# Who builds the gated one-hot rows: half of ScalarE's instructions in the gates stage are replaced by VectorE instructions of two operations

## The chip, the cores and the metric

The kernel runs on one core of one Trainium2 chip, and the metric is the device time of a run in microseconds. The engines named below are TensorE (PE in the profile, PEld its weight loads), VectorE (DVE), ScalarE (ACT), GpSimd (POOL, which issues the indirect gathers) and SyncE (SP, which issues the other transfers). Each engine works through its own list of instructions in order and waits for the others by semaphores.

## The reference, cut to what matters

The program is one decoder block for 1024 tokens of width 1024: a time-mixing and an attention branch, then a feed-forward layer with 16384 experts, of which each token uses 8 x 16 = 128. The change lies in that last layer:

```python
e1 = jnp.take_along_axis(i1, ci // PK_TOPK, axis=-1)
e2 = jnp.take_along_axis(i2, ci % PK_TOPK, axis=-1)
ids = (e1 * PK_NKEYS + e2).reshape(T, PK_HEADS * PK_TOPK)
gates = jax.nn.softmax(vals, axis=-1).reshape(T, PK_HEADS * PK_TOPK)
...
act = jnp.einsum('ced,cd->ce', u_tab[idc], xc)
act = jax.nn.gelu(act, approximate=False) * gc
return jnp.einsum('ce,ced->cd', act, v_tab[idc])
```

An expert is a pair (e1, e2) of numbers from 0 to 127. A token's 128 gates can be written as a 128 x 128 matrix over (e2, e1), zero where the token doesn't use the expert.

## The kernel before

The 1024 tokens are eight tiles of 128. The experts' part of the first four tiles goes by gathering, that of the last four by dense products.

**Gathered tiles, the peers.** `peer` (L806) takes one tile. For each of its 128 choices POOL gathers 128 rows of 4 KB (L792, 512 KB in all) from table u, and DVE multiplies and sums them (L814). Then the same follows from table v (L821). Such a gather with its DVE instruction is called a peer here. There are 1024 of them, one after another in POOL's list, through five buffers called uv. They depend on nothing in the work below, so the framework that schedules the program at build time sets them between the other work.

**Dense tiles.** `choose` (L711) finds the 128 experts and gates of one tile, mostly on DVE. `gates` (L824) turns them into the gate matrices. Tokens are taken in groups of four. For each group DVE makes the one-hot rows of e1 for all four tokens (`oh`, L833). For every eight tokens DVE makes the one-hot rows of e2 (`ohb`, L837, bf16). ACT multiplies each token's e2 row by its gate (`ohg`, L842). PE multiplies `ohg` by `oh` (`gb`, L843), one 128 x 128 product for each token, which the profile shows as two records. ACT moves the group's four products from PSUM to `st` (L844). After eight groups SP stores `st`, 2 MB, in `gd_s` (L847). `st` has two buffers, the PSUM bank of `gb` has two, `ohg` two and `oh` four. A tile has 32 groups, the four tiles 128 groups and 512 `ohg` instructions.

Beside the gates, `ahead` (L854) computes the first 16 of 128 dense products with table u (`ua` on PE, with weights `whi` made by ACT in L153 and `wlo` made by DVE in L154).

`dense` (L861) then walks through the 128 rows of experts. It reads the gates of four rows (`gt`, 1 MB), applies gelu and gate (`gw`, L883 and L884) and makes the products with table v (`yk`, `yr`). DVE takes part in each step (L154, L176, L884, L904). Peers stand between these steps. When the dense steps are over, the peers that are left run alone.

So the list of each engine is: mixing, the choice of experts, the gates stage (from the first `oh` to the first `gw`), the dense stage, and a tail.

Of the kernel before, what the change touches and what calls it, by code (L numbers as in the profile page):

```python
# [13 lines left out]
AF = mybir.ActivationFunctionType  # L14
OP = mybir.AluOpType
# [3 lines left out]
P = 128  # L19
# [28 lines left out]
def body(ctx: ExitStack, tc: tile.TileContext, ins, out, dbg=None):  # L48
    nc = tc.nc
# [15 lines left out]
    def abank(name):  # L65
        return ps.tile([P, 512], F32, name=name, tag="ab", bufs=2)
# [31 lines left out]
    def const(name, shape, dt=F32):  # L98
        t = kp.tile(shape, dt, name=name)
        nc.sync.dma_start(t, ins[name])  # L100
        return t
# [15 lines left out]
    eye_row = const("eye_row", [P, P])  # L117
# [705 lines left out]

    def gates(sp, a, sl, eye8):  # L824

        e1, g = sl[:, 0:P], sl[:, 2 * P:3 * P]
        e2 = sl[:, 3 * P:].bitcast(BF)[:, 0:P]
        nc.scalar.activation(e2, sl[:, P:2 * P], AF.Copy)
        for q in range(0, P, 32):
            st = sp.tile([P, P // CE, 32, CE], F32, name="st", bufs=2)  # L830
            for t in range(0, 32, 4):
                o1 = sp.tile([P, 4, P], F32, name="oh", bufs=4)
                nc.vector.tensor_tensor(o1, eye_row[:, None, :].to_broadcast([P, 4, P]),  # L833
                                        e1[:, q + t:q + t + 4, None].to_broadcast([P, 4, P]), op=OP.is_equal)
                if t % 8 == 0:
                    o2 = sp.tile([P, P, 8], BF, name="ohb", bufs=2)
                    nc.vector.tensor_tensor(o2, eye8, e2[:, None, q + t:q + t + 8].to_broadcast([P, P, 8]),  # L837
                                            op=OP.is_equal)
                b = abank("gb")
                o3 = sp.tile([P, 4, P], F32, name="ohg", bufs=2)  # L840
                for k in range(4):
                    nc.scalar.activation(o3[:, k], o2[:, :, t % 8 + k], AF.Copy, scale=g[:, q + t + k:q + t + k + 1])  # L842
                    nc.tensor.matmul(b[:, k * P:(k + 1) * P], o3[:, k], o1[:, k], start=True, stop=True)  # L843
                nc.scalar.activation(st[:, :, t:t + 4, :].rearrange("p c t f -> p t c f"),  # L844
                                     b.rearrange("p (t c f) -> p t c f", t=4, f=CE), AF.Copy)
            s0 = a * P + q
            nc.sync.dma_start(ins["gd_s"][:, :, s0:s0 + 32, :].rearrange("c p t f -> p c t f"), st)  # L847
# [90 lines left out]
    if "nopeer" not in dbg:  # L938
        with tc.tile_pool(name="sp", bufs=1) as sp:
            eye_f = sp.tile([P, P * 8], F32, name="eye_f", bufs=1)  # L940
            nc.sync.dma_start(eye_f, ins["eye8"])
            eye8 = sp.tile([P, P, 8], BF, name="eye8", bufs=1)
            nc.vector.tensor_copy(eye8.rearrange("p e t -> p (e t)"), eye_f)
            o = W - ND * P
            fh, fl = fh[:, :, o:W], fl[:, :, o:W]
            for a, c in enumerate(late[o // P:]):
                gates(sp, a, choose(*c), eye8)
                ahead(sp, ND * P, fh, fl, range(a * NE // ND, (a + 1) * NE // ND))
            todo += [(c[2], *choose(*c)) for c in late[:o // P]]
        dense(t0 + o, ND * P, fh, fl)  # L950
        for t in todo:
            peer(*t)
# [75 lines left out]
```

## Time and profile before

| | us |
|---|---|
| median of 3 runs (lowest, highest) | 3537.24 (3536.96, 3545.42) |
| the profiled execution, its own time | 3524.41 |
| its span in the trace | 3522.5 |
| busy in the span: PE / DVE / ACT / POOL | 3075.7 / 2923.6 / 1363.1 / 1332.3 |
| first `oh` of the gates stage | 1640.4 |
| last move to `st` starts | 1964.7 |
| first `gw` of the dense stage | 2012.7 |
| last `gw` | 3469.2 |

Times inside the trace count from the span's start. The median of the three runs lies 12.8 us above the profiled execution. Busy shares over the whole span are means over stages with different limits, so the four stretches between the marks in the table are read one by one.

### The profile page before, as it was taken

To read this page: it belongs to the slowest core of one execution; us is meant where nothing else is said; L and a number is where in the kernel's file an instruction comes from. 1 tells how busy PE (TensorE), PEld (TensorE's weight loads), DVE (VectorE), ACT (ScalarE), POOL (GpSimd) and SP (SyncE) were. 2 spreads that over 40 slices of the span, in tenths; PEclk is the share of its full clock that TensorE was granted. 3 is DMA by queue.
4 is the path that set the end of the run, shared out by engine and by line. 5 is a ranking of instruction groups with operands and counts; after the bars stand their busy time and mean duration, and the time that the engine had idled before them with its cause. 6 is when DMAs were issued, how large, how long until landed. Compare 5 with 4: busy or idle time off the path is not lost. (4 is left out here: it accounts for less than half of the span.)

```text
span 3522.5 us, 50906 instructions
## 1 busy us (share of the span) xinstructions
PE 3075.7 (87%) x17382; PEld 2399.4 (68%) x17382; DVE 2923.6 (83%) x6546; ACT 1363.1 (39%) x2506; POOL 1332.3 (38%) x1036
## 2 busy tenths in 40 slices
PE   6999998998778966798888589999999999899994
PEld 5777776776556654676666467777777777777773
DVE  4656558978888878999877689998999999899998
ACT  3444434443424421336989433222223232222321
POOL 0000000025543454411223336655655655556554
PEclk9999999989788987899988799999999999999997
DMA  4222444257675789854678989999999999999997
GB/s 129 76 75 72 121 162 155 83 165 239 217 255 178 253 293 311 289 183 136 208 215 279 323 314 342 353 349 341 348 343 351 348 350 354 348 344 357 340 336 270
DMA packets 407524, 898.68 MB, mean 255 GB/s; under 512 B 69024, under 2 KB 140000, under 8 KB 403168
## 3 DMA queue, kind: packets, MB, share of 16 engines
q0 software_dynamic: 147456, 536.94, 43.7%
q1 hardware_dynamic: 259808, 358.49, 30.2%
q8 instruction: 137, 2.24, 0.3%
q14 instruction: 123, 1.01, 0.1%
HBM read 829.22 MB, written 66.07 MB: 254 GB/s over the span
## 5 line engine op out<-in xcount | busy, mean ns | idle before, releaser
L792 POOL DMA_INDIRECT uv<-u,ids x512 | 663.8, 1296 | 1259.3 <-DVE uv L814 622.4
L792 POOL DMA_INDIRECT uv<-v,ids x512 | 667.4, 1304 | 534.3 <-DVE acc L821 379.8
L821 DVE SCALAR_TENSOR_TENSOR acc<-uv,act,acc 128x1024 f32<-128x1024 f32 x512 | 655.5, 1280 | 63.8 <-DMA uv<-v,ids 57.2
L814 DVE SCALAR_TENSOR_TENSOR uv<-uv,hb 128x1024 f32<-128x1024 f32 x512 | 615.6, 1218 | 74.1 <-DMA uv<-u,ids 73.5
L153 ACT ACTIVATE whi<-wraw 128x512 fp32r<-128x512 f32 x552 | 344.2, 629 | 702.2 <-PE z L169 205.5
L168 PE MATMUL ua<-fh,whi 128*128 128x512 f32 x1024 | 427.8, 418 | 95.2 <-DVE accd L904 71.8
L154 DVE TENSOR_TENSOR wlo<-wraw,whi 128x512 fp32r<-128x512 f32 x552 | 373.3, 684 | 140.4 <-ACT whi L153 129.8
L169 PE MATMUL ua<-fl,whi 128*128 128x512 f32 x1024 | 421.5, 412 | 0.0
L175 ACT ACTIVATE ah<-gw 128x512 fp32r<-128x512 f32 x128 | 80.8, 631 | 657.2 <-DVE gw L884 657.2
L179 PE MATMUL yk<-vh,ah 128*128 128x512 f32 x768 | 305.3, 398 | 21.8 <-DMA gw<-a_s 18.1
L168 PEld LDWEIGHTS ua<-fh,whi 128*128 128x128 f32 x1024 | 203.6, 199 | 160.8 <-DVE accd L904 91.8
L180 PE MATMUL yk<-vl,ah 128*128 128x512 f32 x768 | 305.2, 397 | 7.6 <-DVE vl L176 7.5
L181 PE MATMUL yk<-vh,al 128*128 128x512 f32 x768 | 304.9, 397 | 1.3 <-DVE al L176 1.3
L168 PE MATMUL z<-hh,whi 128*128 128x512 f32 x672 | 275.5, 411 | 1.0 <-ACT whi L153 1.0
L172 PE MATMUL z<-hh,wlo 128*128 128x512 f32 x672 | 274.5, 409 | 0.6 <-DVE wlo L154 0.6
L169 PE MATMUL z<-hl,whi 128*128 128x512 f32 x672 | 274.6, 409 | 0.0
L172 PE MATMUL ua<-fh,wlo 128*128 128x512 f32 x1024 | 264.7, 399 | 6.2 <-DVE wlo L154 6.2
L843 PE MATMUL gb<-oh,ohg 128*128 128x128 f32 x1024 | 227.5, 343 | 42.4 <-ACT ohg L842 41.9
L843 PEld LDWEIGHTS gb<-oh,ohg 128*128 128x128 f32 x1024 | 167.0, 210 | 105.7 <-ACT ohg L842 69.3
L169 PEld LDWEIGHTS ua<-fl,whi 128*128 128x128 f32 x1024 | 203.8, 199 | 43.7
L842 ACT ACTIVATE ohg<-ohb,sl 128x128 f32<-128x128 bf16 x512 | 230.1, 551 | 1.9 <-DVE ohb L837 1.9
L172 PEld LDWEIGHTS ua<-fh,wlo 128*128 128x128 f32 x1024 | 195.0, 191 | 49.9 <-DVE wlo L154 7.1
(320 smaller groups left out, 5672.3 us busy)
## 6 DMA issues: line engine op xcount, KB each, us to landing
wraw<-ut SPq DMA_DIRECT2D x256, 256.0 KB, 6.3
vraw<-v SPq DMA_DIRECT2D x256, 256.0 KB, 6.6
wraw<-w_in SPq DMA_DIRECT2D x168, 256.0 KB, 2.8
gd_s<-st SPq DMA_DIRECT2D x16, 2048.0 KB, 12.4
gt<-gd_s SPq DMA_DIRECT2D x32, 1024.0 KB, 9.2
wraw<-wq SPq DMA_DIRECT2D x64, 256.0 KB, 2.8
g_s<-sgo SPq DMA_DIRECT2D x32, 256.0 KB, 2.7
wraw<-proj SPq DMA_DIRECT2D x32, 256.0 KB, 4.2
```

Of the source, the lines that this page charges most:

```text
L153: nc.scalar.activation(hi, raw, AF.Copy)
L154: nc.vector.tensor_tensor(lo, raw, hi.bitcast(F32), op=OP.subtract)
L168: nc.tensor.matmul(o, hi, xh(k), start=(k == 0), stop=False)
L169: nc.tensor.matmul(o, hi, xl(k), start=False, stop=False)
L172: nc.tensor.matmul(o, lo, xh(k), start=False, stop=(k == n - 1))
L179: nc.tensor.matmul(o, ah, bh, start=first, stop=False)
L180: nc.tensor.matmul(o, ah, bl, start=False, stop=False)
L181: nc.tensor.matmul(o, al, bh, start=False, stop=last)
L792: nc.gpsimd.indirect_dma_start(out=t, out_offset=None, in_=ins[src], in_offset=bass.IndirectOffsetOnAxis(ap=ids[:, j:j + 1], axis=0))
L814: nc.vector.scalar_tensor_tensor(u, u, 1.0, hb, op0=OP.mult, op1=OP.mult, accum_out=act[:, j:j + 1])
L821: nc.vector.scalar_tensor_tensor(acc, v, act[:, j:j + 1], acc, op0=OP.mult, op1=OP.add)
L843: nc.tensor.matmul(b[:, k * P:(k + 1) * P], o3[:, k], o1[:, k], start=True, stop=True)
```

## The change

For each group of four tokens, ACT still makes the `ohg` rows of the first two. For the other two, one DVE instruction (L849, TENSOR_SCALAR) compares the row 0..127 with the token's e2 and multiplies the outcome by its gate, both being per-partition operands. `ohb` now holds only the tokens that ACT needs. One `ohb` instruction of the same size so serves 16 tokens and not eight, and it reads e2 in pairs that are four tokens apart.

```diff
-                if t % 8 == 0:
+                if t % 16 == 0:
+
                     o2 = sp.tile([P, P, 8], BF, name="ohb", bufs=2)
-                    nc.vector.tensor_tensor(o2, eye8, e2[:, None, q + t:q + t + 8].to_broadcast([P, P, 8]),
-                                            op=OP.is_equal)
+                    pairs = e2[:, q + t:q + t + 16].rearrange("p (a b) -> p a b", b=4)[:, :, 0:2]
+                    nc.vector.tensor_tensor(o2.rearrange("p e (a b) -> p e a b", b=2),
+                                            eye8.rearrange("p e (a b) -> p e a b", b=2),
+                                            pairs[:, None].to_broadcast([P, P, 4, 2]), op=OP.is_equal)
                 b = abank("gb")
                 o3 = sp.tile([P, 4, P], F32, name="ohg", bufs=2)
                 for k in range(4):
-                    nc.scalar.activation(o3[:, k], o2[:, :, t % 8 + k], AF.Copy, scale=g[:, q + t + k:q + t + k + 1])
+                    s = slice(q + t + k, q + t + k + 1)
+                    if k < 2:
+                        nc.scalar.activation(o3[:, k], o2[:, :, t % 16 // 2 + k], AF.Copy, scale=g[:, s])
+                    else:
+                        nc.vector.tensor_scalar(o3[:, k], eye_row, e2f[:, s], g[:, s], op0=OP.is_equal, op1=OP.mult)
                     nc.tensor.matmul(b[:, k * P:(k + 1) * P], o3[:, k], o1[:, k], start=True, stop=True)
```

The framework schedules the whole program anew, so the order of the engines' lists changes too. The lists are the same up to the first gate.

ACT in the gates of a tile, before: four `ohg`, then the move to `st` of an earlier group.

```order
L842 ACTIVATE ohg<-ohb,sl 128x128 x3
L844 ACTIVATE st<-gb 128x4x32x4
L842 ACTIVATE ohg<-ohb,sl 128x128 x4
L844 ACTIVATE st<-gb 128x4x32x4
L842 ACTIVATE ohg<-ohb,sl 128x128 x4
```

The same place now, one period of four groups:

```order
L847 ACTIVATE ohg<-ohb,sl 128x128 x4
L851 ACTIVATE st<-gb 128x4x32x4
L847 ACTIVATE ohg<-ohb,sl 128x128 x2
L851 ACTIVATE st<-gb 128x4x32x4
L847 ACTIVATE ohg<-ohb,sl 128x128 x2
L851 ACTIVATE st<-gb 128x4x32x4 x2
```

ACT has two `ohg` for each move to `st`, and once in four groups two moves to `st` stand together.

DVE in the gates of a tile, before. Steps of the next tile's `choose` (L765 to L773) and peers (L814) stand between those of the gates:

```order
L769 TENSOR_TENSOR oh<-oh,te 128x2048
L837 TENSOR_TENSOR ohb<-eye_14365,sl 128x1024
L833 TENSOR_TENSOR oh<-eye_row,sl 128x512
L771 TENSOR_TENSOR oh<-oh 128x8x128
L833 TENSOR_TENSOR oh<-eye_row,sl 128x512
L771 TENSOR_TENSOR oh<-oh 128x8x64
L837 TENSOR_TENSOR ohb<-eye_14365,sl 128x1024
L833 TENSOR_TENSOR oh<-eye_row,sl 128x512
L771 TENSOR_TENSOR oh<-oh 128x8x32
L814 SCALAR_TENSOR_TENSOR uv,act<-uv,hb 128x1024
```

The same place now:

```order
L849 TENSOR_SCALAR ohg<-eye_row,sl 128x128 x2
L833 TENSOR_TENSOR oh<-eye_row,sl 128x512
L849 TENSOR_SCALAR ohg<-eye_row,sl 128x128 x2
L833 TENSOR_TENSOR oh<-eye_row,sl 128x512
L839 TENSOR_TENSOR ohb<-eye_14365,sl 128x1024
L849 TENSOR_SCALAR ohg<-eye_row,sl 128x128 x2
```

Nothing but the gates stands there any more. The next tile's `choose` and PE's `ua` products follow in a piece of their own, between one tile's gates and the next one's.

DVE at the end of the program, before: the last peers stand one by one between the closing steps of the dense tiles (L193 to L195 and L803).

```order
L821 SCALAR_TENSOR_TENSOR acc<-uv,act,acc 128x1024
L803 SCALAR_TENSOR_TENSOR accd<-accd,rsw,fnw 128x1024
L194 TENSOR_TENSOR rsw<-rsw 128x1
L821 SCALAR_TENSOR_TENSOR acc<-uv,act,acc 128x1024
L195 SCALAR_TENSOR_TENSOR rsw<-rsw 128x1
```

The same place now:

```order
L195 SCALAR_TENSOR_TENSOR rsw<-rsw 128x1
L821 SCALAR_TENSOR_TENSOR acc<-uv,act,acc 128x1024
L803 SCALAR_TENSOR_TENSOR accd<-accd,rsw,fnw 128x1024
L821 SCALAR_TENSOR_TENSOR acc<-uv,act,acc 128x1024 x45
L187 TENSOR_SCALAR rsw<-ssqf 128x1
```

Forty-five peers in a row now stand behind the last closing step. Counted over DVE's list, the 1024 peers are spread like this:

| peers | before | changed |
|---|---|---|
| ahead of the first `oh` | 283 | 283 |
| from the first `oh` to the first `gw` | 83 | 20 |
| between the first and the last `gw` | 640 | 646 |
| after the last `gw` | 18 | 75 |

## Rows read from the trace of the kernel before

**Rows 1.** Four stretches: length, busy PE, PEld, DVE, ACT, POOL; clock, DMA share, GB/s.

```profile
1640.00:1966.00 326.00, 275.34 (x1227) 203.33 (x1226) 267.08 (x627) 303.78 (x681) 79.83 (x66) 0.90 0.73 225
1966.00:2012.70 46.70, 16.49 (x60) 12.67 (x58) 23.62 (x40) 7.24 (x12) 20.47 (x17) 0.68 0.92 329
2012.70:3469.20 1456.50, 1370.89 (x5728) 1092.28 (x5729) 1348.35 (x1799) 426.06 (x737) 835.32 (x640) 0.98 0.95 344
3469.20:3522.50 53.30, 8.24 (x34) 5.68 (x32) 41.71 (x102) 6.79 (x12) 16.97 (x15) 0.62 0.76 264
```

**Rows 2.** Groups by line in 1640 to 1966: count, busy us, mean ns, idle before.

```profile
L842 ACT ACTIVATE ohg<-ohb,sl 128x128 f32<-128x128 bf16 x512 | 230.1, 551 | 1.9 <-DVE ohb L837 1.9
L843 PE MATMUL gb<-oh,ohg 128*128 128x128 f32 x1024 | 227.5, 343 | 42.4 <-ACT ohg L842 41.9
...
L814 DVE SCALAR_TENSOR_TENSOR uv<-uv,hb 128x1024 f32<-128x1024 f32 x67 | 80.9, 1218 | 3.5 <-DMA uv<-u,ids 3.5
...
L844 ACT ACTIVATE st<-gb 128x512 f32<-128x512 f32 x128 | 79.1, 618 | 2.9 <-PE gb L843 1.6
```

**Rows 3.** Waits in 1640 to 1966: total us, times, longest.

```profile
POOL uv L792 <- DVE uv L814: 252.3, 49, 39.2
```

**Rows 4.** ACT's timeline in the gates of the first tile: start us, us.

```profile
1690.85 0.72 ACT L844 ACTIVATE st<-gb 128x512 f32<-128x512 f32 x1
1691.33 1.90 ACT L842 ACTIVATE ohg<-ohb,sl 128x128 f32<-128x128 bf16 x4
1692.99 0.73 ACT L844 ACTIVATE st<-gb 128x512 f32<-128x512 f32 x1
```

**Rows 5.** PE's timeline, four 128 x 128 products in a row (eight records).

```profile
1600.39 1.15 PE L694 MATMUL s<-keyt,pq 128*128 128x128 f32 x8
```

**Rows 6.** DVE's timeline: `ohb` and the next instruction, TENSOR_SCALAR and the next.

```profile
1690.30 0.69 DVE L837 TENSOR_TENSOR ohb<-eye,sl 128x1024 bf16<-128x1024 bf16 x1 [0.56 <-ACT ohg L842]
1690.90 0.69 DVE L833 TENSOR_TENSOR oh<-eye_row,sl 128x512 f32<-128x512 f32 x1
1691.51 0.29 DVE L771 TENSOR_TENSOR oh<-oh 128x256 bf16<-128x256 bf16 x1
...
1625.50 0.23 DVE L747 TENSOR_SCALAR d<-d 128x128 uint32<-128x128 f32 x1
1625.65 0.28 DVE L737 TENSOR_TENSOR gate<-gate,gsum 128x128 f32<-128x128 f32 x1
```

**Rows 7.** The dense stage by line on DVE, 2012.7 to 3469.2.

```profile
L821 DVE SCALAR_TENSOR_TENSOR acc<-uv,act,acc 128x1024 f32<-128x1024 f32 x366 | 468.8, 1281 | 38.0 <-DMA uv<-v,ids 32.4
L814 DVE SCALAR_TENSOR_TENSOR uv<-uv,hb 128x1024 f32<-128x1024 f32 x274 | 328.7, 1220 | 49.2 <-DMA uv<-u,ids 48.7
```

**Rows 8.** One stretch with a whole `choose` ahead of the first `oh`; columns as in Rows 1.

```profile
1611.00:1640.40 29.40, 23.22 (x95) 18.39 (x94) 27.76 (x126) 12.99 (x18) 0.94 (x1) 0.88 0.40 131
```

**Rows 9.** Transfers of the page: count, KB each, median us to landing.

```profile
gd_s<-st SPq DMA_DIRECT2D x16, 2048.0 KB, 12.4
gt<-gd_s SPq DMA_DIRECT2D x32, 1024.0 KB, 9.2
```

**Rows 10.** From the last store of gates to the first `gw`: SP's and DVE's timeline.

```profile
1965.32 0.36 SPq L847 DMA_DIRECT2D gd_s<-st  x1
...
2012.69 1.12 DVE L884 TENSOR_TENSOR gw<-gw,gt 128x512 f32<-128x512 f32 x1 [0.25 <-ACT gw L883]
```

**Rows 11.** The same store among the transfers issued in 1960 to 1970.

```profile
gd_s<-st SPq DMA_DIRECT2D x1, 2048.0 KB, 23.7
```

**Rows 12.** Peers in a row: DVE's timeline with four, POOL's gap between two gathers.

```profile
3439.31 5.24 DVE L821 SCALAR_TENSOR_TENSOR acc<-uv,act,acc 128x1024 f32<-128x1024 f32 x4
...
3488.51 1.14 POOL L792 DMA_INDIRECT uv<-v,ids  x1 [0.30 <-issue]
```

**Rows 13.** A stretch of gates with no `ua` products, as in Rows 1.

```profile
1708.00:1712.00 4.00, 3.76 (x16) 3.13 (x15) 2.59 (x6) 3.87 (x10) 3.30 (x3) 0.50 0.98 343
```

More of the change, by code (lines that the diff above doesn't have):

```diff
@@ L824, in gates @@
     def gates(sp, a, sl, eye8):
-        e1, g = sl[:, 0:P], sl[:, 2 * P:3 * P]
+        e1, e2f, g = (sl[:, i * P:(i + 1) * P] for i in range(3))
         e2 = sl[:, 3 * P:].bitcast(BF)[:, 0:P]
-        nc.scalar.activation(e2, sl[:, P:2 * P], AF.Copy)
+        nc.scalar.activation(e2, e2f, AF.Copy)
         for q in range(0, P, 32):
```

## The prediction, written before the changed kernel was run

> **What bounds the kernel now.** I read the span in four stretches first [rows 1], because the shares of the whole span mix them. In the gates stage (1640 to 1966) ACT is busy for 303.8 of 326 us, PE for 275 and DVE for 267: ACT sets the pace. In the dense stage (2012.7 to 3469.2) ACT is nearly idle, PE has 1371, DVE 1348 of 1456.5 us and the DMA engines 95%. A saving on ACT can only count in the first stretch.
>
> The groups of the gates stage come next [rows 2]. The reader is to see that the 512 `ohg` (230 us) and the 128 moves to `st` (79 us) make up ACT's time, and that PE's idle time ahead of the products is put down to `ohg`. DVE also ran 67 peers there. POOL waited 252 us for DVE to give back a `uv` buffer [rows 3], so DVE's order, not POOL, decided how many peers fitted in.
>
> ACT's timeline gives the period of a group [rows 4]: move to move is 1692.99 - 1690.85 = 2.14 us. A move holds ACT for 0.48 us until the next `ohg` starts. Four `ohg` take 1.90 us, the last of them 0.55 [rows 2], so one follows another after (1.90 - 0.55) / 3 = 0.45. From the last `ohg` to the next move it is 2.14 - 0.48 - 3 x 0.45 = 0.31.
>
> **The change part by part.** Removed: 256 `ohg` on ACT and 32 of 64 `ohb` on DVE. Added: 256 TENSOR_SCALAR on DVE. Moved: `choose` and the `ua` products leave the gates, and 63 peers leave the gates stage.
>
> ACT per group: 0.48 + 0.45 + 0.31 = 1.24 us. Two waits come on top, from the new order, in which a move to `st` follows its products more closely. Four products take 1.15 us [rows 5], 0.29 each. After its second `ohg` starts, a group needs 0.55 + 3 x 0.29 = 1.42 us until its products are done. The second of two adjacent moves would start 0.31 + 0.48 = 0.79 us after that `ohg`, so it waits 0.63 us once in four groups. The first move of each period stands two `ohg` later, at 2 x 0.45 + 0.31 = 1.21 us, and waits 0.21 us. That is (0.63 + 0.21) / 4 = 0.21 more, 1.45 us. In three of the four tiles about a third of the groups have no adjacent moves, so I take 1.38 us. Bounds: 1.24 without waits, 2.14 as now.
>
> DVE per group: `oh` 0.60 us from start to start [rows 6], two TENSOR_SCALAR and a quarter of `ohb`. No TENSOR_SCALAR with two per-partition operands is in the trace. The nearest row has constants, has the same 128 columns and takes 0.15 us from start to start [rows 6]. The peer of table v, with a per-partition operand, takes 0.06 us longer than that of table u without one [rows 7], so I take 0.20. The far bound is 0.60, a 512-column instruction. `ohb` took 0.60; in pairs it may run at the rate of `oh`, twice as long for its 1024 elements, 1.21. I take 0.80. Sum: 0.60 + 0.40 + 0.20 = 1.20 us (1.05 to 2.10), just under ACT, so the added work is hidden by ACT's 1.38. Without that cover each 0.1 us would cost 13 us over 128 groups.
>
> By the Trainium skill (Vector Engine (DVE) Microarchitecture Reference, section 5.2, Measured stream behaviour) a port keeps its full rate only while a stream has runs of at least two neighbouring 4-byte words, and a source that hops at each word takes 1.73 instead of 1.05 ns a column. The pairs of e2 are such single words. By that `ohb` would take an estimated 512 x 0.68 ns = 0.35 us more; no row here shows the pattern, and it makes the third rival below likelier.
>
> Gates of four tiles: 128 x 1.38 = 177 us.
>
> Between two tiles' gates DVE now runs a whole `choose` with seven `wlo` and two peers, and PE runs its `ua`. Such a piece stands in the trace ahead of the first `oh`: 29.4 us, 27.8 of it busy on DVE, with one `choose`, eight `wlo` and one peer [rows 8]. With a second peer it is 30.6 us. DVE starts it before ACT has drained a tile's gates; about as long passes at the start of the next gates until the first `ohg`, so I let these two cancel. Three pieces: 92 us. Bounds: 25 each, without the second peer and its idle time and with more of the start overlapped, and 35 each, because on SP the `wraw` loads of `ua` now stand behind all four stores of a tile: 75 to 105.
>
> From the last gate to the first `gw` the trace shows 2012.69 - 1965.32 = 47.4 us [rows 10], since 64 `ua` products and 22 peers stood there. Now 13 peers are left, and the time is the last store, the first `gt` and about 2 us for gelu and multiply. A store lands in 12.4 us, `gt` in 9.2 [rows 9], but the last store, among gathers, took 23.7 [rows 11]. That is 24 to 35 us; I take 30.
>
> Gates stage, first `oh` to first `gw`: 177 + 92 + 30 = 299 us, against 2012.7 - 1640.4 = 372.3 now. Gain: 73 us.
>
> Then the peers come back. The dense stage gets 6 more, 646 for 640. DVE is 93% busy there, with peers waiting for their gathers [rows 1, 7]. At 1.28 us each [rows 7] that is +8 us (0 if PE covers them; 14 at the stage's 1456.5 / 640 = 2.28 us).
>
> The tail gets 57 more, 75 for 18, with nothing beside them. Four in a row take 5.24 us on DVE, 1.31 each; POOL needs 1.14 + 0.30 = 1.44 for a gather [rows 12], and the dense stage's 2.28 is the far bound. I take 1.40, between the two rows of peers in a row: +80 us (75 to 130).
>
> Sum: -73 + 8 + 80 = +15 us. The profiled execution took 3524.4 us, 1.9 beyond its span, and would take 3539; the median shown lies 12.8 above it, so I forecast 3537.2 + 15 = 3552 us.
>
> A second count agrees. From 1640 on, DVE's instructions run nearly back to back in both kernels, and the change adds 256 x 0.20 = 51 us and takes away 64 x 0.60 - 32 x 0.80 = 13: +38 us on DVE. It must win idle time back elsewhere to break even, and it only does so behind the last gate.
>
> **The rivals.**
>
> *Faster.* The new waits on ACT are hidden, and a group takes 1.24 us: 159 instead of 177. DVE does its pieces in 26 us each (-14), and the tail's peers run at 1.31 (-5): +15 - 18 - 14 - 5 = -22, 3515 us. For it speaks that ACT waited only 1.6 us for products so far [rows 2]. Against it: only 1.6 of the 29.4 us of such a piece are idle on DVE [rows 8]. The Trainium skill (ScalarE: Activation LUTs, Rules for kernel authors) says that a multiply belongs on VectorE rather than ScalarE; by that rule the change goes this way.
>
> *Slower: TensorE's clock falls in the gates.* In a stretch of gates without `ua` the granted clock was 0.50, the lower level of 1.2 GHz, and PE was busy for 3.76 us with two groups, 1.88 each [rows 13]. Today's period of 2.14 hides that; 1.38 does not, and now all gates run without `ua` beside them. If half the groups run so: 64 x 0.50 = 32 us more, +47, 3584 us. It decides from the point where a group takes PE more than ACT. Against it: PE gets its work more densely than today.
>
> *Slower: DVE becomes the bound.* With TENSOR_SCALAR at 0.30 and `ohb` at 1.21 a group takes 0.60 + 0.60 + 0.30 = 1.50, with some waits 1.60: 128 x 0.22 = 28 us more, +43, 3580 us.
>
> *The gates don't shorten as they should, because of the stores.* A store follows every eight groups and there are two `st` buffers; were each store awaited for its 12.4 us [rows 9], 16 of them would make 198 us: +21, in all +36, 3573 us. Against it: gathers and stores shared the DMA engines so far, and few gathers run beside the gates now.
>
> **How the numbers follow.** Chances: forecast 0.45, faster 0.30, clock 0.10, DVE 0.09, stores 0.06. A measurement of this kernel can tell about 0.3% from no change, 10.6 us. The forecast's own range is -5 to +35 us, 3532 to 3572: 0.60 of it is slower by over 0.3%, 0.38 within, 0.02 faster. Of the faster case 0.75 is over 0.3%, 0.25 within; the others are slower but for a little. Faster: 0.45 x 0.02 + 0.30 x 0.75 = 0.23. Within: 0.45 x 0.38 + 0.30 x 0.25 = 0.25. Slower: 0.52. The range reaches from a faster case with its transition at 24 us and the peers of the dense stage covered, 3515 - 6 - 8 = 3501, to the clock's case, 3584, and a little beyond, because two of the slower cases may meet: 3501 to 3592.
>
> **What would show each step right or wrong.** In the trace after: the move-to-move period of ACT in the gates (1.38 us; 1.24 for the faster case); TENSOR_SCALAR at 0.20 from start to start and `ohb` at 0.80; PE's granted clock in the gates; about 30 us between the last `oh` of one tile and the first of the next; first `gw` near 1940 rather than 2013; 75 peers behind the last `gw` at 1.40 us each. The forecast is wrong if the first `gw` comes before 1915, or if the tail's peers take under 1.2 or over 1.7 us.

## The result: slower, by less than DVE's added work

The changed kernel takes 3571.93 us (median of 4 runs, 3568.43 to 3584.34) against 3537.31 for the kernel before (4 runs): +34.6 us. The ratio is 1.0097, with a 95% interval of 1.0075 to 1.0119. The forecast was 3552 us with a range of 3501 to 3592, and slower the likeliest side.

### The profile page after: what moved, and what is told of

The parts are those of the page before. It is cut to its first block, busy times and chain, and to the rows that moved or that the text cites. A ratio compares the mean times of both kernels' runs of the same rounds, so it can differ in the third digit from the quotient of the medians.

```text
span 3566.5 us, 51000 instructions
## 1 busy us (share of the span) xinstructions
PE 3022.2 (85%) x17382; PEld 2380.2 (67%) x17382; DVE 2970.2 (83%) x6770; ACT 1261.1 (35%) x2250; POOL 1331.1 (37%) x1036
## 4 chain that ended last, share of the span: by engine, by line
PE 35%; issue 20%; DVE 18%; DMA 14%; POOL 10%; ACT 2%; SPq 0%; POOLq 0%; DVEq 0%; ACTq 0%
POOL uv L792 10%; DMA uv<-v,ids 7%; PE gb L850 4%; PE z L169 4%; PE z L168 4%; DMA uv<-u,ids 4%; PE z L172 3%; DVE uv L814 3%; DVE acc L821 2%; DVE wlo L154 2%; PE ua L172 1%; PE ua L168 1%; PE ua L169 1%; PE sc L527 1%; DVE gw L891 1%
## 5 line engine op out<-in xcount | busy, mean ns | idle before, releaser
L792 POOL DMA_INDIRECT uv<-u,ids x512 | 672.2, 1313 | 1335.5 <-DVE uv L814 481.6
L792 POOL DMA_INDIRECT uv<-v,ids x512 | 657.8, 1285 | 509.8 <-DVE acc L821 352.2
L814 DVE SCALAR_TENSOR_TENSOR uv<-uv,hb 128x1024 f32<-128x1024 f32 x512 | 615.7, 1219 | 77.3 <-DMA uv<-u,ids 73.5
L179 PEld LDWEIGHTS yk<-vh,ah 128*128 128x128 f32 x768 | 145.1, 189 | 71.4 <-ACT ah L175 35.9
L850 PE MATMUL gb<-oh,ohg 128*128 128x128 f32 x1024 | 160.2, 297 | 32.5 <-ACT ohg L847 32.4
L180 PEld LDWEIGHTS yk<-vl,ah 128*128 128x128 f32 x768 | 145.2, 189 | 47.2 <-DVE vl L176 12.3
```

The costliest lines, as they stand in the source:

```text
L179: nc.tensor.matmul(o, ah, bh, start=first, stop=False)
L180: nc.tensor.matmul(o, ah, bl, start=False, stop=False)
L792: nc.gpsimd.indirect_dma_start(out=t, out_offset=None, in_=ins[src], in_offset=bass.IndirectOffsetOnAxis(ap=ids[:, j:j + 1], axis=0))
L814: nc.vector.scalar_tensor_tensor(u, u, 1.0, hb, op0=OP.mult, op1=OP.mult, accum_out=act[:, j:j + 1])
```

## The profile after

The profiled execution took 3568.43 us, its span is 3566.5. These are the stretches up to the first `oh`, to the last move to `st`, to the first `gw`, to the last `gw` and to the end (columns as in Rows 1):

```profile
0.00:1652.80 1652.80, 1416.54 (x10340) 1097.88 (x10341) 1244.42 (x3981) 619.04 (x1068) 372.70 (x300) 0.91 0.55 179
1652.80:1929.40 276.60, 226.82 (x1283) 183.50 (x1281) 246.10 (x740) 207.29 (x433) 9.08 (x8) 0.95 0.57 169
1929.40:1959.60 30.20, 0.00 (x0) 0.00 (x0) 13.70 (x25) 2.56 (x4) 15.31 (x13) 0.54 0.96 346
1959.60:3418.60 1459.00, 1370.69 (x5729) 1093.14 (x5730) 1351.64 (x1868) 425.46 (x737) 844.80 (x645) 0.98 0.95 344
3418.60:3566.50 147.90, 8.12 (x33) 5.64 (x31) 114.37 (x159) 6.79 (x12) 89.19 (x72) 0.55 0.85 298
```

The same first two stretches of the kernel before, cut at its own marks:

```profile
0.00:1640.40 1640.40, 1405.16 (x10341) 1085.79 (x10342) 1242.89 (x3982) 619.61 (x1068) 379.73 (x300) 0.92 0.55 180
1640.40:1964.70 324.30, 273.64 (x1220) 201.94 (x1218) 266.21 (x626) 302.08 (x678) 78.83 (x65) 0.89 0.73 225
```

The reader is to see four things. The stage from the first `oh` to the first `gw` is 306.8 us instead of 372.3: 65.5 gained. The dense stage is 2.5 longer. The tail is 147.9 instead of 53.3 [rows 1]: 94.6 lost. Together that is +31.6 us. The spans differ by 44, because the part ahead of the first `oh` is 12.4 longer; there the change has moved nothing. Nine of the executions profiled below and above run the same 283 peers ahead of the gates, and their first `oh` stands anywhere between 1640.4 and 1662.4. The one of before is the earliest of them, so these 12 us are put down to the execution and not to the change.

DVE gives a second way to add up. From the first `oh` to the end it was busy for 1680.7 us before (266.2, 24.4 behind the last move, 1348.4, 41.7) and for 1725.8 after (246.1 + 13.7 + 1351.6 + 114.4): +45.1. It was idle for 201.4 and 187.9: -13.5. The sum is again +31.6. The idle time moved as well. In the gates it fell from 58.1 to 30.5 us, from there to the first `gw` from 23.6 to 16.5, and in the tail it rose from 11.6 to 33.5. So of the 94.6 us that the tail grew by, 72.7 are work of DVE and 21.9 are idle time; its waits for gathers there grew from 4.5 us to 26.6.

In the gates the groups of instructions that answer to [rows 2] are these (count, busy us, mean ns, idle before):

```profile
L850 PE MATMUL gb<-oh,ohg 128*128 128x128 f32 x1024 | 160.2, 297 | 32.5 <-ACT ohg L847 32.4
...
L847 ACT ACTIVATE ohg<-ohb,sl 128x128 f32<-128x128 bf16 x256 | 117.1, 519 | 5.1 <-DVE ohb L839 5.1
...
L849 DVE TENSOR_SCALAR ohg<-eye_row,sl 128x128 f32<-128x128 f32 x256 | 76.9, 342 | 27.7 <-PE gb L850 25.4
L851 ACT ACTIVATE st<-gb 128x512 f32<-128x512 f32 x128 | 75.9, 593 | 20.2 <-PE gb L850 20.2
...
L839 DVE TENSOR_TENSOR ohb<-eye,sl 128x1024 bf16<-128x1024 bf16 x32 | 21.9, 684 | 0.0
```

The moves to `st` now wait 20.2 us for products, where they waited 1.6, and DVE waits 25.4 us for products before it writes a row of `ohg`. ACT's timeline shows one period of four groups, from a move at 1684.62 to the one at 1690.83 (start us, us, and in brackets the idle time before):

```profile
1684.62 0.60 ACT L851 ACTIVATE st<-gb 128x512 f32<-128x512 f32 x1 [0.54 <-PE gb L850]
1685.11 1.75 ACT L847 ACTIVATE ohg<-ohb,sl 128x128 f32<-128x128 bf16 x4
1687.06 0.60 ACT L851 ACTIVATE st<-gb 128x512 f32<-128x512 f32 x1 [0.20 <-PE gb L850]
1687.56 0.92 ACT L847 ACTIVATE ohg<-ohb,sl 128x128 f32<-128x128 bf16 x2
1688.39 0.58 ACT L851 ACTIVATE st<-gb 128x512 f32<-128x512 f32 x1
1688.86 0.94 ACT L847 ACTIVATE ohg<-ohb,sl 128x128 f32<-128x128 bf16 x2
1689.71 0.58 ACT L851 ACTIVATE st<-gb 128x512 f32<-128x512 f32 x1
1690.83 0.60 ACT L851 ACTIVATE st<-gb 128x512 f32<-128x512 f32 x1 [0.54 <-PE gb L850]
```

That is 6.21 / 4 = 1.55 us a group, with the two waits that were forecast (0.54 and 0.20 for 0.63 and 0.21). On DVE's timeline two TENSOR_SCALAR hold the engine from 1687.14 to 1687.66, 0.26 each:

```profile
1687.14 0.60 DVE L849 TENSOR_SCALAR ohg<-eye_row,sl 128x128 f32<-128x128 f32 x2 [1.07 <-PE gb L850]
1687.66 0.68 DVE L833 TENSOR_TENSOR oh<-eye_row,sl 128x512 f32<-128x512 f32 x1
```

## The experiments

Each of the three sets below ran on one chip, together with the kernel before, whose median was 3543.24, 3521.88 and 3541.23 us. So the ratios are compared. The changed kernel's is 1.0097, and 0.001 is 3.5 us. The microseconds in the expectations are those of the first comparison, with 3537 for the kernel before.

### First set: buffers, split, place of the peers

**Four `ohg` buffers** (`bufs=2` to `bufs=4` for `o3`).

> The changed kernel with four buffers for `ohg` and not two; on every engine the peers stand where they stood (20 in the gates stage, 646 in the dense stage, 75 in the tail). Question: are the 1.55 us of a group in the gates (6.21 us for four, with the waits of ACT of 0.54 and 0.20 us and one of DVE of 1.07 us for products) a matter of the two buffers? If so, a group falls to DVE's own 1.26 us (0.60 for `oh`, 0.51 for two TENSOR_SCALAR, 0.15 for a quarter of `ohb`), and 128 groups save up to 37 us: 3535 to 3545 us, tail unchanged at about 148 us. Rival: the waits come from the order of moves and products and stay, 3565 to 3575. Second rival: something else (PE, the stores, two PSUM banks) takes over near 1.45, 3555 to 3562.

Measured: 3573.31 us, ratio 1.0095 (1.0067 to 1.0124). The rival holds: in the gates ACT still waits 0.54 us once in a period, and the period is 5.90 us (moves at 1683.80 and 1689.70). The gates get 7 us shorter (269.5), and nothing of it can be told in the run's time.

**One token of four on ACT, three on DVE.**

```diff
-                if t % 16 == 0:
+                if t == 0:
...
-                    if k < 2:
+                    if k < 1:
```

> The changed kernel with one token of four on ACT and three on DVE (one `ohb` for 32 tokens), peers again at the same places (20, 646, 75). DVE's own work for a group rises from 1.26 to 0.60 + 3 x 0.26 + 0.08 = 1.46 us, ACT's falls to about 0.48 + 0.45 + 0.31 - 0.45 = 0.79. If DVE carries the gates of the changed kernel, a group takes 1.46 plus the wait of today, 0.27: 1.73, 128 x 0.18 = +23 us, 3595. If ACT with its waits carries them, the group falls to DVE's 1.46: -12 us, 3560.

Measured: 3579.48 us, ratio 1.0111 (1.0085 to 1.0138), between the two expectations, and not to be told from the changed kernel. The gates take 273.9 us, with DVE busy for 272.1 of them. So the 26 us more that DVE has to do there fit into the 30 us that it was idle in the changed kernel. There a group was thus not paced by DVE's work alone; ACT and DVE take turns at rows and products. The same holds for all that follows the first `oh`; first the changed kernel, then this one (columns as in Rows 1):

```profile
1652.80:3566.50 1913.70, 1605.63 (x7043) 1282.28 (x7041) 1725.81 (x2789) 642.10 (x1184) 958.39 (x736) 0.93 0.89 315
1662.40:3573.50 1911.10, 1600.13 (x7043) 1288.28 (x7041) 1754.10 (x2901) 596.81 (x1055) 956.94 (x736) 0.93 0.89 316
```

DVE works 28.3 us more and the stretch is no longer. So added work on DVE may also go into its idle time and cost nothing. The expected 0.08 us a group for `ohb` was wrong, as the last section shows.

**Peers moved from the tail into the gates, and, in the kernel before, out of the tail.** The peers' DVE instructions from the 284th on, 70 of them (40 in the kernel before), get a priority like that of the first gates:

```diff
...
+            with tc.high_priority(offset=tc.cur_priority - spot[1]):
+                nc.vector.scalar_tensor_tensor(*args, **kw)
```

> The changed kernel, all its instructions the same, with 70 of the peers' DVE instructions given a higher priority in the building of the order: 7 stand ahead of the first gate, 77 in the gates stage, 641 in the dense stage, 16 in the tail (before the change: 0, 83, 640, 18). Theory: the loss is the 57 peers that run alone at 1.66 us in the tail; 59 peers leave it (-98 us), and in the gates they cost at most 1.2 us each (57 x 1.2 = 68), less what they fill of DVE's idle 25 us there, with 8 us for the 7 ahead: -47 to -22, 3525 to 3550 us. Rival: DVE is the bound from the first gate to the end, and the change adds 256 x 0.26 - 32 x 0.60 = 47 us of work to it, wherever the peers stand: within 10 us of the changed kernel, 3562 to 3582.

> The kernel before, all its instructions the same, with 40 of the peers' DVE instructions given a higher priority: 7 ahead of the first gate, 95 in the gates stage, 639 in the dense stage, none in the tail (before: 0, 83, 640, 18). Theory that peers alone in the tail are dear and peers in the gates cheap: 18 peers leave the tail at 1.4 to 1.66 us (-25 to -30); 7 ahead cost 8, and 12 in the gates between 0 (DVE was idle 59 us there) and 14: 3515 to 3534 us. Rival, DVE is the bound from the first gate on: the idle time that is left does not change, 3532 to 3542.

Measured: 3595.48 us, ratio 1.0137 (1.0105 to 1.0169), and for the kernel before without peers in the tail 3557.25 us, 1.0039 (1.0022 to 1.0056). The second missed both of its expectations. The first stands 14 us above the changed kernel by the ratios, outside its rival's 10, though the two intervals overlap. In the first the tail is back at 50.8 us, but the stage up to the first `gw` takes 418.8 us, 112 more than in the changed kernel for 57 peers. In the second the tail falls from 53.3 to 32.3, and the stage grows from 372.3 to 404.9. DVE stood 53.2 us before gathers in the first one's gates.

### Second set: spread peers, and the tail's price

**The same, spread.** One peer behind every second group; in the changed kernel, in a split of three to one, and in the kernel before.

```diff
+        a, i = divmod(seen[0] - 283, 18)
...
+        n = 32 * a + 2 * i + 1
...
+            with tc.high_priority(offset=tc.cur_priority - spot[n]):
```

> The changed kernel with peers brought forward one by one, behind every second group of the gates instead of in a bunch: 7 ahead of the first gate, 55 in the gates stage, 644 in the dense stage, 35 in the tail (the changed kernel: 0, 20, 646, 75; the bunched one: 7, 77, 641, 16). In the bunched kernel a peer moved from the tail saved 1.64 us there (97.1 / 59) and cost 1.96 us in the gates stage (112 / 57), of which 0.93 us was DVE standing before a gather that had not landed. Theory that the bunch was at fault: spread out, the gathers land in time and a peer costs DVE's 1.2 us: 35 x 1.2 = +42, 40 x 1.64 = -66, 7 x 1.2 = +8 ahead of the gates: -16, about 3555 us. Rival: a peer in these gates costs 1.96 us wherever it stands, since gathers share the DMA engines with the 2 MB stores: +69 - 66 + 8 = +11, about 3583 us.

> Three tokens of four on ACT and one on DVE (`ohb` as before the change, one for 8 tokens), with peers brought forward behind every second group: 7 ahead of the first gate, 58 in the gates stage, 642 in the dense stage, 34 in the tail. A group takes ACT 0.48 + 2 x 0.45 + 0.31 = 1.69 us without waits, and DVE 0.60 + 0.26 + 0.30 = 1.16, so DVE has 0.53 us a group to spare, 68 us in 128 groups, for 36 peers brought there (43 us). Theory that peers are free only as far as ACT leaves DVE time: gates 128 x 1.69 = 216, pieces 92, transition 30, so a stage of 338; dense 1457; tail 53 + 16 x 1.64 = 79: 1874 us behind the first gate against 1882 before and 1914 with the change: 3535 to 3550. Rival as in the bunched kernel: each peer in the gates stops DVE for about 0.9 us, 36 x 0.9 = 32 more, 3565 to 3580.

> The kernel before, its peers brought forward behind every second group: 7 ahead of the first gate, 95 in the gates stage (spread over the four tiles), 639 in the dense stage, none in the tail. The same counts with a bunch of 20 in the first tile measured a tail of 32.3 us (-21), a transition of 34.9 (-13), and gates longer by 45.7. Theory that the bunch was at fault: the 25 peers that now stand within the gates and not behind them (18 of the tail, 7 of the transition) cost at most 1.2 us each, less what they fill of DVE's idle 58 us there: -34 + 0 to 25 and 8 ahead: 3517 to 3543 us. Rival, the gates have no room for more: as with the bunch, +8 to +15, 3545 to 3560 us.

Measured ratios: 1.0172 (1.0139 to 1.0204), 1.0153 (1.0119 to 1.0186), 1.0070 (1.0049 to 1.0091). All are slower than the kernel they were made from, as the rivals said, and by somewhat more than they said (in ratios 1.013, 1.012 and 1.006 at most). In the first one's gates DVE waits for gathers about once for every second peer (total us, times, longest):

```profile
DVE uv L798 <- DMA uv<-u,ids: 43.5, 26, 4.8
```

The waits go with the way the peers were moved. Only chosen peers got the higher priority, and a peer of table u may overtake another. So in DVE's list some peers are passed over, and each of them keeps its landed buffer. This is the order of the built program, with the buffers' numbers and the peers alone (28133 was gathered 18 peers before 28187):

```
L798 SCALAR_TENSOR_TENSOR uv_28184,act_28058<-uv_28184,hb_28059 128x1024
L798 SCALAR_TENSOR_TENSOR uv_28187,act_28058<-uv_28187,hb_28059 128x1024
L800 SCALAR_TENSOR_TENSOR uv_28133,act_28058<-uv_28133,hb_28059 128x1024
```

Of the 55 peers in that gates stage, 38 ran while three or four of the five buffers were held in this way; in the bunched kernel it was 60 of 77, in the split of three to one 40 of 58, in the two kernels made from the one before 30 of 95 (three buffers) and 54 of 95 (mostly one). With one or two buffers left, a gather is issued just ahead of its use: the peer at 1688.82 in the spread kernel used the gather issued at 1680.03. DVE's timeline, read together with this order up to the first `gw`, ties the waits to the held buffers: in the spread kernel 26 waits, 43.6 us in all, stand ahead of the 38 peers, and 8 waits, 6.9 us, ahead of the other 17. In the bunched kernel it is 44 waits, 53.2 us, ahead of the 60, and 7 waits, 7.8 us, ahead of the other 17. Slower transfers, the spread kernel's rival, don't show: a gather there landed in 4.8 us in the median, in the gates of the kernel before in 6.6. In the spread kernel made from the one before, gathers stopped DVE for only 13.7 us up to the first `gw`, so there the waits explain a part of the loss at most. In all other kernels here, the changed one too, no peer is passed over. So these five runs do not tell what a peer in its right order costs in the gates. Whether the changed instructions with peers moved in order would beat the kernel before was not tried and stays open.

**Half rows in the tail.** The last 75 peers gather 2 KB a row and add up half the columns.

> The changed kernel; the last 75 peers, those of the tail, gather half a row each (2 KB and not 4 KB, from another place of the table) and add up 512 columns and not 1024, so half of their sum is left out; the order is the same (20, 646, 75). Question: what sets the 1.66 us of a peer in the tail? If the bytes do (0.52 MB in 1.66 us is 316 GB/s, the DMA engines 85% busy), a peer falls to what POOL takes to issue a gather, 1.02 + 0.30 = 1.32 us or a little more: 57 to 75 x 0.3 = 17 to 23 us less, tail 125 to 131 us, 3549 to 3556. If the turn-round of five buffers or POOL's issue does, whatever the bytes, the tail stays within 8 us of 148, 3564 to 3574. If DVE's 1.2 us does, a peer falls to the 1.32 of POOL as well, but DVE's waits for gathers in the tail (26.6 us now) say that it doesn't.

Measured: 3529.84 us, ratio 1.0016 (0.9998 to 1.0034), with the tail at 119.2 us. First POOL's timeline in the changed kernel's tail, then in this one's:

```profile
3503.67 1.01 POOL L792 DMA_INDIRECT uv<-v,ids  x1 [0.30 <-issue]
3504.98 1.02 POOL L792 DMA_INDIRECT uv<-v,ids  x1 [0.30 <-issue]
3506.31 1.02 POOL L792 DMA_INDIRECT uv<-v,ids  x1 [0.30 <-issue]
3507.63 1.98 POOL L792 DMA_INDIRECT uv<-v,ids  x1 [0.30 <-DMA uv<-v,ids]
```

```profile
3514.25 1.11 POOL L792 DMA_INDIRECT uv<-v,ids  x1 [0.30 <-issue]
3515.66 1.17 POOL L792 DMA_INDIRECT uv<-v,ids  x1 [0.30 <-issue]
3517.13 1.14 POOL L792 DMA_INDIRECT uv<-v,ids  x1 [0.30 <-issue]
```

And a stretch of each tail with peers alone, in the same sequence (columns as in Rows 1):

```profile
3489.00:3549.00 60.00, 0.00 (x0) 0.00 (x0) 46.55 (x37) 0.00 (x0) 46.63 (x36) 0.50 0.90 311
```

```profile
3470.00:3520.00 50.00, 0.00 (x0) 0.00 (x0) 29.36 (x42) 0.00 (x0) 39.02 (x37) 0.50 0.71 210
```

With half the bytes a gather follows another after 1.35 us in the mean (37 in 50 us), and POOL hardly waits for anything but its own issue. With whole rows 36 gathers take 60 us, 1.67 each, at 311 GB/s and 90% busy DMA engines, and POOL's spans lengthen now and then, some behind a landing. DVE is busy for only 46.55 of these 60 us and waits for gathers. So neither POOL's issue nor DVE's own work alone sets the price of a peer with whole rows. That the bytes do is likely but not shown by itself: DVE's instruction was halved with them, and its part was not separated. The tail fell by more than was expected, 28.7 us for 75 peers, 0.38 each.

### Third set: one half of the change at a time, and POOL

**The relief of ACT alone, the load on DVE alone.** The first leaves out the 256 TENSOR_SCALAR and multiplies by a constant matrix for their tokens, the second adds them to the kernel before.

```diff
-                        nc.vector.tensor_scalar(o3[:, k], eye_row, e2f[:, s], g[:, s], op0=OP.is_equal, op1=OP.mult)
-                    nc.tensor.matmul(b[:, k * P:(k + 1) * P], o3[:, k], o1[:, k], start=True, stop=True)
+                        pass
+                    nc.tensor.matmul(b[:, k * P:(k + 1) * P], o3[:, k] if k < 2 else ident, o1[:, k], start=True, stop=True)
```

```diff
+                idle = sp.tile([P, 2, P], F32, name="idle", bufs=2)
+                for k in range(2):
+                    s = slice(q + t + k, q + t + k + 1)
+                    nc.vector.tensor_scalar(idle[:, k], eye_row, sl[:, P:2 * P][:, s], g[:, s], op0=OP.is_equal, op1=OP.mult)
```

> The relief of ACT alone: the changed kernel without its 256 TENSOR_SCALAR; for two tokens of four PE multiplies by a constant matrix in place of the gated rows, so their gates are left out. DVE has 256 x 0.26 = 66 us less to do. The order puts 36 peers in the gates stage, 643 in the dense stage and 62 in the tail (the changed kernel: 20, 646, 75; before: 83, 640, 18). Theory that the change loses because DVE's added work has to be paid: nearly all of it comes back, 45 to 66 us less than the changed kernel, 0.990 to 0.997 of before. Rival, the loss is the place of the peers, and that depends on ACT's relief alone: the gates stay at 277 us, paced by ACT, PE and the 0.54 us waits, and only 13 peers leave the tail at 1.65 us: 21 us less than the changed kernel, 1.003 of before.

> The load on DVE alone: the kernel before, and beside it 256 TENSOR_SCALAR of the kind that the change adds, written to a tile that nobody reads; ACT makes all four rows as before. The order puts 32 peers in the gates stage, 646 in the dense stage, 63 in the tail (before: 83, 640, 18). If DVE's work is what is paid: the tail grows by 45 x 1.65 = 74 us, and the stage, which ACT's 302 us of work still hold up, shrinks by 20 to 30 with the peers gone from it: about +47 us, 1.011 to 1.016 of before. Rival: DVE had 58 us to spare in those gates, which take the 66 us in: 1.000 to 1.004.

Measured: 3510.69 us, ratio 0.9914 (0.9885 to 0.9943), and 3637.11 us, 1.0274 (1.0248 to 1.0300). The stretches from the first `oh` on, as above; the relief alone:

```profile
1659.20:1885.80 226.60, 209.09 (x1271) 175.35 (x1270) 198.64 (x511) 197.75 (x428) 27.10 (x22) 0.98 0.76 228
1885.80:1923.30 37.50, 2.93 (x13) 2.06 (x11) 17.49 (x29) 4.65 (x8) 18.35 (x14) 0.59 1.05 396
1923.30:3382.40 1459.10, 1368.00 (x5723) 1089.76 (x5724) 1349.72 (x1850) 424.03 (x737) 849.45 (x642) 0.98 0.95 343
3382.40:3508.90 126.50, 9.32 (x39) 6.77 (x37) 97.92 (x146) 6.79 (x12) 74.40 (x58) 0.55 0.82 291
```

The load alone:

```profile
1657.90:2004.10 346.20, 286.70 (x1283) 208.35 (x1281) 283.83 (x795) 306.02 (x687) 26.22 (x20) 0.94 0.51 149
2004.10:2038.70 34.60, 0.00 (x0) 0.00 (x0) 14.78 (x26) 3.09 (x5) 15.73 (x13) 0.55 1.00 367
2038.70:3502.90 1464.20, 1372.63 (x5722) 1095.56 (x5723) 1352.12 (x1857) 425.61 (x737) 836.16 (x644) 0.97 0.95 342
3502.90:3632.50 129.60, 9.45 (x40) 7.00 (x38) 99.00 (x147) 6.79 (x12) 79.22 (x60) 0.55 0.83 292
```

| TENSOR_SCALAR on DVE | ACT makes all four rows | ACT makes two |
|---|---|---|
| none | 1 (before) | 0.9914 |
| 256 | 1.0274 | 1.0097 (the change) |

The kernels on the right also have half of `ohb` on DVE, those on the left all of it.

In the first of the two the first theory holds. Without the TENSOR_SCALAR the changed kernel is 0.0183 of before faster, 65 us, for 66 us of work taken from DVE, although 62 peers still stand in the tail. From the first `oh` on DVE is busy for 1663.8 us there and idle for 185.9, against 1725.8 and 187.9 in the changed kernel: the length differs by the work. The gates lose 50 us (226.6 for 276.6) and the tail 21, while the piece between gates and first `gw` gains 7. Leaving the rows out does a second thing, though: half of the products need not wait for a row from DVE. This run does not separate the two. ACT's relief, with the halved `ohb`, is worth 30 us by itself; DVE's work is 16.9 us less than before, its idle time 15.5 less.

The load without the relief costs 97 us, more than either side expected, and there nothing reads the added rows: 45 more peers go to the tail (+76 us), and the stage, where ACT is busy for 306 of 346 us, gives nothing back (380.8 for 372.3). DVE's work from the first `oh` on is 69.0 us more than before, and its idle time 23.5 more. So the added work costs time by itself; that it costs more than its length here is not explained further.

**The rows on POOL.** One token of four, with three on ACT; then two of four, in place of DVE's (the edit of the second):

```diff
-                        nc.vector.tensor_scalar(o3[:, k], eye_row, e2f[:, s], g[:, s], op0=OP.is_equal, op1=OP.mult)
+                        nc.gpsimd.tensor_scalar(o3[:, k], eye_row, e2f[:, s], g[:, s], op0=OP.is_equal, op1=OP.mult)
```

> One token of four goes to POOL (the same TENSOR_SCALAR, issued there), three stay on ACT, none goes to DVE; `ohb` as before. The order: 49 peers in the gates stage, 644 in the dense stage, 48 in the tail. DVE has no more to do than before the change, ACT 1.69 us a group. If POOL makes its row in under 1.7 us and DVE's work is what counts, the gates take 128 x 1.69 = 216 and three pieces of 26, the transition 30: a stage of 325 to 335 us (-42), a tail of 53 + 30 x 1.65 = 103 (+49), dense +5: 1.003 of before, between 0.999 and 1.007. Rival: POOL's rows are slow or hold up the gathers and DVE (no trace so far shows such an instruction on POOL): over 1.010.

> The changed kernel with its 256 TENSOR_SCALAR on POOL and not on DVE. The order: 32 peers in the gates stage, 646 in the dense stage, 63 in the tail. DVE has 32 x 0.60 = 19 us less than before the change. If POOL makes a row in under 0.7 us, the gates keep their 277 us or less, the stage takes 305, and the tail 53 + 45 x 1.65 = 127: -67 + 8 + 74 = +15, less what the lighter DVE gives back in the pieces, 1.000 to 1.005 of before. Rival: a row takes POOL 1 us or more, two of them pace a group at over 2 us, and the gathers stand behind them: over 1.012.

Measured: 3565.94 us, ratio 1.0074 (1.0049 to 1.0099), between expectation and rival, and 3624.33 us, 1.0238 (1.0213 to 1.0263), as the rival said. On POOL's timeline five such rows in a line take 5.67 us, 1.13 each (start us, us; the kernel with two on POOL):

```profile
1699.20 5.67 POOL L849 TENSOR_SCALAR ohg<-eye_row,sl 128x128 f32<-128x128 f32 x5
```

DVE needs 0.26. With two on POOL a group takes at least 2.26 us, more than ACT took for four. None of the versions that leave nothing out beats the kernel before.

## Why the forecast came out as it did

**The direction was right, and the second count gave its reason.** That count says that DVE's added work has to be paid, because DVE has little idle time behind the first gate, and the third set bears it out for this change. It came to +38 us; with the measured 0.26 and 0.60 it is 256 x 0.26 - 32 x 0.60 = +47, and DVE's busy time shows +45. Where it said that idle time is won back only behind the last gate, it was wrong: most was won in the gates (27.6 us), some behind them (7.1), and the tail gave 21.9 back. And it is no rule for every added row: with one token on ACT and three on DVE, 28.3 us more of DVE's work went into idle time.

**The sum by stretches was too low by 17 us, from two terms that were too small and two that were too large.** That it missed by no more is partly luck: the first two were 31 us too small together, and the other two took 14 of that back.

- *ACT per group, 1.38 us, 177 in all:* mis-sized. The gates without the pieces between tiles take 276.6 - 83.3 = 193.3 us, 1.51 a group: +16. The two waits came as forecast (0.54 and 0.20). What lies between them was too small: without the waits the period is 6.21 - 0.74 = 5.47 us, 1.37 a group, where the forecast had 1.24. In part that is the move ahead of a waiting move, which holds ACT for its whole 0.58 us and not for 0.48. So the steady group is 1.55 and not 1.45, and the tiles without adjacent moves did not bring the mean down to 1.38: from the first `oh` of a tile to its last it is 47.2 us in each of the first three tiles, whatever the pattern of moves.
- *DVE's rows hidden by ACT's 1.38, no price in the gates:* this overlap did not hold. Without the rows the gates take 226.6 us and not 276.6. With half as many again they take 273.9, so it is not DVE's busy time alone. That products wait for rows from DVE, and DVE for products, is the likely part; no run separates it.
- *DVE per group, 1.20 us:* near, 0.60 + 2 x 0.26 + 0.15 = 1.27. TENSOR_SCALAR took 0.26 and not 0.20. `ohb` in pairs took 0.60 from start to start (1689.37 to 1689.97), as before, and not 0.80. By the Trainium skill (Vector Engine (DVE) Microarchitecture Reference, section 5.2, Measured stream behaviour) the hop from one 4-byte word to the next would have cost `ohb` an estimated 0.35 us; at 684 ns for 688 the trace doesn't show it, for pairs of bf16 that fill a word.
- *Pieces, 3 x 30.6 = 92 us:* 28.2, 26.9 and 28.2 us between the last `oh` of one tile and the first of the next, 83.3 in all: -9, within the bounds.
- *Transition, 30 us:* 30.2. The stage is so 306.8 us for 299.
- *Dense stage, +8:* +2.5; PE's work covered most of the six peers.
- *Tail, 57 x 1.40 = +80:* the other mis-sized term, 94.6, or 1.66 each, just under the 1.7 that the forecast had named as a sign of being wrong. 1.40 is near the price of POOL's issue, and the half rows run at 1.35. Whole rows run slower, with the DMA engines 90% busy at 311 GB/s. The forecast had taken its price between two rows, DVE's and POOL's, and had no term for the transfers themselves.

**The rivals.** *Faster* failed at its first condition: the waits of ACT were not hidden. *The clock falls:* no. The granted clock in the gates rose to 0.95 from 0.89, near the level of 2.4 GHz; it is low (0.54 and 0.55) only behind the gates and in the tail, where PE has little or nothing to do. *DVE becomes the bound:* not in the gates, where DVE was idle for 30 of 277 us, a group took 1.51 and more work on DVE fitted in; but over the whole of what follows the first gate DVE was the right engine to look at. *Stores:* nothing in the waits of the gates points to `st`.

**What stays open:** what a peer in its gathered order would cost in the new gates; by which part of the halved peer, bytes or DVE, the tail with half rows fell; how much of the 65 us is DVE's work and how much the products' waits for its rows; and why the load without the relief costs more than its length.

## What to carry to other kernels

When work goes from the engine that paces one stage to an engine that is busy through the rest of the program, look at the second engine's whole remaining list: add up its busy and its idle time from the change to the end, beside the sum by stages. Here the 256 rows on DVE had to be paid nearly in full, while 128 more went into idle time and cost nothing that could be told. Work that filled idle slots of a stage loses its shelter once the stage gets shorter, and it comes back where it runs alone, here at 1.66 us a peer and not at the 1.28 that DVE needs for it. Work brought forward out of order may hold the buffers that it skips, so look at the order of the buffers before believing such a test.

## What had not been expected of the hardware

- `ohb` of the same 1024 elements, with e2 read in pairs of bf16 four tokens apart, took 684 ns, as with eight in a row. Read as single bf16 values four tokens apart, in the kernel with one token on ACT, it took 1222:

```profile
L839 DVE TENSOR_TENSOR ohb<-eye,sl 128x1024 bf16<-128x1024 bf16 x16 | 19.6, 1222 | 0.0
```

- A TENSOR_SCALAR of 128 columns with two per-partition operands holds POOL for 1.13 us and DVE for 0.26, 4.3 to 1. The Trainium skill (GPSIMD Engine Reference, section 3.1, Elementwise — side-by-side cycle accounting) has about 2 to 1, for an add of two tensors of 2048 columns; this other instruction, at 128 columns, had twice that ratio.
- While POOL made such rows, the same `oh` on DVE took longer, 727 ns in the mean for 684. The median is only 693 (684 in the changed kernel), so it is some that took much longer, up to 946. The kernel with two rows on POOL:

```profile
L833 DVE TENSOR_TENSOR oh<-eye_row,sl 128x512 f32<-128x512 f32 x128 | 92.3, 727 | 104.4 <-PE gb L850 99.7 <-ACT sl L781 4.2 <-issue 0.2
```

- Executions with the same lists up to the first gate reached it at 1640.4 to 1662.4 us, on several chips, and those of the third set, on one chip, at 1649.6 to 1659.2: marks of one profile in the span differ by up to 22 us without any change.
